# Second expert's weights into the staging tiles, fourth expert's into the tile of the MoE stage freed last, and two small ScalarE stores moved behind a copy

## The chip, the cores and the metric

The kernel runs on one core of a Trainium2 chip, as one launch. The metric is device time in microseconds, the median of the runs shown. Engines are named as in the profile: PE (matmul) with PEld (its weight loads), DVE (VectorE), ACT (ScalarE), POOL (GpSimd) and SP (SyncE, which issues most DMAs). "ACTq", "SPq" and "POOLq" are the queues of these engines where they issue a DMA.

## What is computed

Two layers of a transformer-like trunk on 512 latent and 256 context tokens of width 1024. Each layer has a mixer (projections, a convolution, a state-space scan, an output projection), and then a mixture of experts, which is the part that matters here:

```
t = modulate(rms_norm(h, g_ffn), shift, scale)          # (tokens, 1024)
g_sel = argmax(t @ w_rg + b_rg)                         # one of 4 groups
top_v, top_i = top_k(softmax(expert logits in g_sel), 2)
comb[e, t] = weight of expert e for token t             # two of 16 experts per token
for e in 16 experts:                                    # SwiGLU, hidden width 256
    hid = silu(t @ w_gate[e]) * (t @ w_up[e])
    out += comb[e][:, None] * (hid @ w_down[e])
h = h + gate * out
```

All is float32. Layer 0 routes all 768 tokens, layer 1 (the last) only the 512 latent ones. At the end one RMS norm of the latent tokens is the output.

## The kernel before

**Routing and blocks.** The kernel computes only what the routing chose. Token rows are written to a table in HBM (`h2d`, by `Pair.store`, L1036). From the logits DVE works out which tokens go to which expert; blocks of at most 128 tokens are fetched from `h2d` by an indirect DMA of POOL (`gather`, L1282), turned on PE (`turned`, L1288), copied from PSUM by ACT (first half) and DVE (second half) in `turn` (L1297, the copies are L1301), multiplied by gate and up (`up`, L1315), by silu (`swiglu`, L1309), turned again (`turn_hid`), multiplied by down (`down`, L1343) and added into `acc_d` in HBM by an indirect DMA (`scatter`).

**Experts.** Experts 0, 1 and 2 are "static": their blocks come first, whatever the routing, and they are multiplied in plain float32 straight from the loaded weights. The other 13 come in an order that the routing sets (a register holds the expert's number; `expert`, L1365), and their weights are split into a high and a low part (`split_load`, L1265): ACT casts the loaded piece to the high part (L1275), DVE or POOL subtract for the low part (L1276), and the next expert's piece is loaded in its place. The text calls the fourth expert in order, the first dynamic one, e3, and the next e4.

**Pieces and tiles.** An expert's weights come in six pieces of 512 KB (`load_piece`, L1113): 0 and 1 gate, 2 and 3 up, 4 and 5 down. The tiles are these: `raw0` to `raw5` are the six staging tiles of 4 KB a partition; `HC0`, `HC1` hold expert 0's gate and up; `HL0` and `HL1` are two large tiles (four pieces each) that hold the mixer's activations until the last output projection; `wp` and `wraw` hold down pieces; `C01`, `wraw`, `HL0`, `HL1`, `HC0`, `HC1` later hold high and low parts.

Before, expert 0's gate and up go to HC0 and HC1 and its down to raw4 and raw5; expert 1's gate and up to HL1; expert 2's to HL0; e3's to raw0 to raw3. The large loads after `pr.store` are placed behind the last store by `with behind(pr.stored)` (L1141). e3's pieces are loaded at L1479, once SP has read the number of the expert.

**What sets the order.** The tile framework schedules the program from the source order and its own estimate of time, and each engine then runs its own list strictly in order. Every hardware DMA, from whichever queue, takes the next of eight semaphores in turn; its issue waits until the DMA that had the same semaphore eight places before has landed. So an issue can hold an engine's queue, and everything behind it on that engine, until an unrelated transfer has landed.

**The overflow table.** `loop_rows` (L1457) writes a small table for blocks beyond the planned ones: PE turns it, ACT copies it (L1465), and two stores are issued on ACT's queue, `ovd` (L1468) and `ebd` (L1469). `ebd` needs only `ebi`, which DVE has ready before the first block starts. The loop that reads the table stands at the end of the MoE stage (L1510).

Of the kernel before, what the change touches and what calls it, by code (L numbers as in the profile page):

```python
# [8 lines left out]
F32 = mybir.dt.float32  # L9
# [9 lines left out]
P = 128  # L19
D = 1024  # L20
# [23 lines left out]
def places(caps):  # L44

    static, dyn = caps
    nd = sum(n > P for n in dyn)
    seq, single = [(e, True, n) for e, n in enumerate(static)], list(range(nd, len(dyn)))
    for p in range(nd):
        seq.append((p, False, dyn[p]))  # L50
        k = 0 if p == nd - 2 else -(-len(single) // (nd - p - (p < nd - 2)))
        seq += [(q, False, dyn[q]) for q in single[:k]]
        single = single[k:]
    out, b, row = [], 0, 0
    for p, static, n in seq:
        out.append((p, static, b, row, n))
        b += -(-n // P)
        row += n
    return out
# [3 lines left out]
def hybrid_kernel(ctx: ExitStack, tc: tile.TileContext, x, c, ctxt, c_ctx, w_ada, b_ada, g_mix, g_ffn,  # L63
# [3 lines left out]
    nc = tc.nc  # L67
    V, G, S, T = nc.vector, nc.gpsimd, nc.scalar, nc.tensor

    const = ctx.enter_context(tc.tile_pool(name="const", bufs=1))  # L70
    main = ctx.enter_context(tc.tile_pool(name="main", bufs=1))
# [4 lines left out]
    @contextmanager  # L76
    def behind(*inss):

        with ExitStack() as st:
            for ins in inss:  # L80
                st.enter_context(tc.issue_after(ins.ins))
            yield
# [4 lines left out]
    def tp_tile():  # L87
        return psum.tile([P, 512], F32, name="tp")

    def sm_tile():  # L90
        return psum.tile([P, 512], F32, name="sm")
# [100 lines left out]
    for l in range(2):  # L192
        for p, static, b, row, n in places(CAPS[l]):
            j = p + NE - NS if static else p
# [305 lines left out]
    for l in range(2):  # L500
# [312 lines left out]
        for c in (4, 5, 0, 3, 1, 2):  # L813
            xw = main.tile([P, 2, 512], F32, name="t4", bufs=8)
            G.tensor_mul(v4(xw), hview(xs[:, c, :])[:, None].to_broadcast([P, 2, NH, 64]), both(ex[:, 1], c, 64))
            pt = tp_tile()
# [17 lines left out]
        for i in range(1, 5):  # L834
            for d in range(2):
                c0, c1 = chain[d][i - 1], chain[d][i]
                t = mixp.tile([P, 512], F32, name="Y", bufs=3)
# [231 lines left out]
        def save_x1(i0):  # L1069
            for i in (i0, i0 + 1):  # L1070
                nc.sync.dma_start(out=chunk(acc_d, i + 1), in_=X1[:, :, i, :])
# [21 lines left out]
        items, M_x = places(CAPS[l]), MAXOV[l]  # L1093
# [19 lines left out]
        def load_piece(e, j, t=None):  # L1113

            if t is None:
                t = moep.tile([P, D], F32, name=f"raw{j}")
            w = (w_gate, w_up, w_down)[j // 2]
            src = w[l][e] if isinstance(e, int) else w[l][ds(e, 1)].rearrange("a r f -> (a r) f")
            src = src.rearrange("(p k) f -> p k f", p=P)
            n = src.shape[1] // 2  # L1120
            nc.sync.dma_start(out=t.rearrange("p (k f) -> p k f", k=n), in_=src[:, n * (j % 2):n * (j % 2) + n, :])
            return t


        raw, gu, dn = {}, {}, {}
        t = [main.tile([P, 2048], F32, name=f"HC{q}") for q in range(2)]
        for j in range(4):
            load_piece(0, j, t[j // 2][:, j % 2 * D:j % 2 * D + D])
        gu[0], dn[0] = [t], [[load_piece(0, j) for j in (4, 5)]]
        before = moep.tile([P, 16, 16], F32, name="before")  # L1130
        G.affine_select(out=before, in_=ones[:, 0:1, None].to_broadcast([P, 16, 16]), pattern=[[1, 16], [-1, 16]],
                        compare_op=OP.is_gt, fill=0.0, base=0, channel_multiplier=0)
# [4 lines left out]
        pr.store(nc.sync)  # L1137
        pr.finish()

        t = [main.tile([P, 4, D], F32, name=f"HL{q}") for q in (1, 0)]  # L1140
        with behind(pr.stored):  # L1141
            gu[1] = [[load_piece(1, j, t[0][:, j]) for j in range(4)]]
            dn[1] = [[load_piece(1, j, main.tile([P, D], F32, name="wp", bufs=2)) for j in (4, 5)]]
            if last:
                save_x1(2)
            gu[2] = [[load_piece(2, j, t[1][:, j]) for j in range(4)]]
            t = main.tile([P, 2, D], F32, name="wraw", bufs=3)
            dn[2] = [[load_piece(2, j, t[:, j - 4]) for j in (4, 5)]]


        def rt(name, *shape, dt=F32):
            return moep.tile([P, *shape], dt, name=name)
# [71 lines left out]
        for e in range(NS):  # L1224
# [3 lines left out]
            pt = sm_tile()  # L1228
# [68 lines left out]
        def turn(xg, n, whole):  # L1297
            if whole:
                x = main.tile([P, K8, P], F32, name="t4", bufs=8)[:, :, :n]
                for (ks, pt), copy in zip(turned(xg, n), (S.copy, V.tensor_copy)):  # L1300
                    copy(x[:, ks, :], pt)  # L1301
                return [x]
            xh, xl = [main.tile([P, K8, P], F32R, name="t4", bufs=8)[:, :, :n] for _ in range(2)]
            for ks, pt in turned(xg, n):
                S.copy(xh[:, ks, :], pt)
                V.tensor_sub(xl[:, ks, :], pt, xh[:, ks, :])
            return xh, xl
# [57 lines left out]
        def expert(i):  # L1365
            p, static = items[i][:2]
            return p if static else nc.sync.value_load(eidi[0:1, p:p + 1], min_val=NS, max_val=NE - 1)
# [89 lines left out]
        def loop_rows():  # L1457

            ov = rt("ov", 2, M_x)
            V.tensor_copy(ov[:, 0], idx[:, NB:])  # L1460
            V.tensor_copy(ov[:, 1], cw[:, NB:])
            pt = tp_tile()
            T.transpose(pt[0:2 * M_x, 0:P], ov.rearrange("p q b -> p (q b)"), ident)
            ovT = main.tile([P, P], F32, name="diag", bufs=2)[0:2 * M_x]
            S.copy(ovT, pt[0:2 * M_x, 0:P])  # L1465
            ovd = dram.tile([2 * M_x, P], F32, name=f"ovd{l}")
            ebd = dram.tile([M_x, 1], I32, name=f"ebd{l}")
            nc.scalar.dma_start(out=ovd, in_=ovT)  # L1468
            nc.scalar.dma_start(out=ebd.rearrange("b o -> o b"), in_=ebi[:, :M_x])  # L1469
            return ovd[0:M_x], ovd[M_x:2 * M_x], ebd  # L1470

        blocks = [(i, items[i][2] + j, j == 0) for i in range(NE) for j in range(-(-items[i][4] // P))]
# [3 lines left out]
        whole = lambda w: len(w) == 1  # L1476
        ninc, eidi, bf, rf = slots()
        e3, e4 = expert(3), expert(4)
        raw[3] = [load_piece(e3, j) for j in range(4)]  # L1479
        xT = turn(xgs.pop(0), size[0], whole(gu[0]))  # L1480
        hid, prev_i = None, None
        for i, b, new in blocks:
            if b + 2 == NS:
                idx, cw, ebi = slot_tokens()
# [18 lines left out]
            if new and i == 4:  # L1503
                idxd, cwd, ebd = loop_rows()
# [61 lines left out]
    for i in range(4):  # L1566
        xf = combine(i)
        ss = sml.tile([P, 8], F32, name="ss")
        o = main.tile([P, D], F32, name="t4", bufs=8)
# [36 lines left out]
```

## Time and profile before

| what | value |
|---|---|
| median of 3 runs | 1329.05 us (1326.38 to 1335.55) |
| the profiled execution's own time | 1326.32 us |
| its span, first to last instruction | 1324.6 us |
| PE busy | 1081.6 us (82%) |
| DVE, POOL, ACT busy | 879.0, 611.0, 552.3 us |
| moved by DMA | 259.82 MB, mean 196 GB/s |
| mean granted TensorE clock | 0.912 |

The profile is of one execution. The MoE stage of layer 0 lies from about 473 to 720 us of the span, that of layer 1 from about 1054 to 1300. In each, a routing part (PE nearly idle, DVE at work on small tables, the DMA engines loading weights) is followed by the blocks. A granted clock of 1.00 is 2.4 GHz and 0.50 is 1.2 GHz, its two levels. In a timeline a row gives the start in us, the busy time in us, the engine and line, the operation with its tiles, and in brackets how long the engine sat idle before it and what ended that. A matmul of float32 operands shows as two records, so `x8` of L1320 in the trace is `x4` in the program's order.

### The profile page before, as it was taken

Reading aid. Unit: us, or ns where it says so; the run is one execution under the profiler, and the core shown is the slowest. Engines: PE = TensorE matmul, PEld = TensorE weight load, DVE = VectorE, ACT = ScalarE, POOL = GpSimd, SP = SyncE. Lnnn points to the kernel's source line nnn. Section 1 sums busy time; section 2 is a strip of 40 time slices with the busy share of each in tenths; the row PEclk is TensorE's granted clock in tenths of the full one; section 3 lists DMA queues with packets and bytes.
Section 4 is the critical chain, followed back from the end, with each engine's and each line's share of the span. In section 5 each row is a group of like instructions: output and inputs, shape, how many; then the busy total and the mean of one; then the engine's idle time right before and its main releaser. Section 6 shows DMA issues by size and latency. Waiting matters only on the chain. (4 is left out here: it accounts for less than half of the span.)

```text
span 1324.6 us, 19405 instructions
## 1 busy us (share of the span) xinstructions
PE 1081.6 (82%) x7091; PEld 880.8 (66%) x7091; DVE 879.0 (66%) x1326; ACT 552.3 (42%) x993; POOL 611.0 (46%) x463
## 2 busy tenths in 40 slices
PE   3889697697879958999997498998888948998881
PEld 1567575566769946888885475976667936787750
DVE  3459997668776474477662679975877473476872
ACT  3522243334682322476652422233654212366641
POOL 1427485347683010376763135233865111378761
PEclk9989798897999977999999699889898978999996
DMA  8865433553445175799995746013575275799974
GB/s 265 272 174 182 148 128 91 186 198 95 125 151 139 43 273 199 227 344 333 319 315 112 257 152 217 11 49 121 182 257 204 60 273 202 211 324 315 320 234 138
DMA packets 121360, 259.82 MB, mean 196 GB/s; under 512 B 15968, under 2 KB 61646, under 8 KB 116142
## 3 DMA queue, kind: packets, MB, share of 16 engines
q1 hardware_dynamic: 110852, 227.19, 50.4%
q0 software_dynamic: 8032, 27.14, 8.9%
q10 hardware_dynamic: 2377, 4.22, 0.8%
q8 instruction: 57, 0.93, 0.3%
q14 instruction: 42, 0.34, 0.1%
HBM read 228.05 MB, written 30.47 MB: 195 GB/s over the span
## 5 line engine op out<-in xcount | busy, mean ns | idle before, releaser
L464 POOL TENSOR_TENSOR t<-wp,t 128x1024 fp32r<-128x1024 f32 (+1 forms) x36 | 109.3, 3037 | 149.5 <-ACT t L463 132.9
L723 DVE SCALAR_TENSOR_TENSOR acc<-v,cwcol,acc 128x448 f32<-128x448 f32 (+19 forms) x176 | 131.5, 778 | 0.6
L481 PE MATMUL mm<-HL,t 128*128 128x512 f32 (+1 forms) x272 | 110.6, 409 | 9.3 <-ACT t L463 6.2
L1275 ACT CAST wraw<-raw 128x1024 fp32r<-128x1024 f32 x84 | 87.1, 1049 | 56.7 <-DMA raw<-in_w_gate_dram 21.1
L483 PE MATMUL mm<-HL,t 128*128 128x512 f32 (+1 forms) x272 | 106.6, 392 | 2.2 <-POOL t L464 2.2
L482 PE MATMUL mm<-HL,t 128*128 128x512 f32 (+1 forms) x272 | 107.8, 396 | 0.2 <-DVE HL L376 0.2
L1362 POOL DMA_INDIRECT acc_d<-t,idx x38 | 66.1, 1740 | 84.7 <-issue 22.1
L354 POOL TENSOR_TENSOR rstd<-ms,mhalf 128x1 f32<-128x1 f32 (+3 forms) x29 | 24.5, 846 | 158.8 <-DVE ms L352 134.5
L1284 POOL DMA_INDIRECT t<-h2d,idx x38 | 47.1, 1239 | 95.0 <-PE sm L1320 31.2
L652 DVE SCALAR_TENSOR_TENSOR t<-t,pcol,t 128x772 f32<-128x772 f32 (+1 forms) x64 | 86.9, 1358 | 1.9
L482 PE MATMUL sm<-C,t 128*128 128x256 f32 (+8 forms) x288 | 81.2, 282 | 4.2 <-DVE C L1276 2.5
L481 PE MATMUL mm<-t,HL 128*128 128x256 f32 x256 | 77.0, 301 | 8.6 <-ACT t L644 2.3
L481 PE MATMUL sm<-wraw,t 128*128 128x256 f32 (+8 forms) x288 | 83.6, 290 | 0.0
L1276 POOL TENSOR_TENSOR HL<-raw,HL 128x1024 fp32r<-128x1024 f32 x24 | 64.6, 2725 | 39.1 <-ACT HL L1275 33.7
L483 PE MATMUL sm<-wraw,t 128*128 128x256 f32 (+8 forms) x288 | 80.9, 281 | 0.0
L463 ACT CAST t<-wp 128x1024 fp32r<-128x1024 f32 (+1 forms) x40 | 42.1, 1054 | 90.3 <-DMA wp<-in_w_in_dram 40.0
L483 PE MATMUL mm<-t,HL 128*128 128x256 f32 x256 | 75.3, 295 | 0.1
L482 PE MATMUL mm<-t,HL 128*128 128x256 f32 x256 | 75.2, 294 | 0.0
L1276 POOL TENSOR_TENSOR C<-raw,wraw 128x1024 fp32r<-128x1024 f32 x24 | 62.6, 2620 | 20.6 <-ACT wraw L1275 19.4
L481 PEld LDWEIGHTS mm<-HL,t 128*128 128x128 f32 x272 | 53.5, 198 | 27.0 <-ACT t L463 8.0
L482 PE MATMUL sm<-HL,t 128*128 128x256 f32 (+8 forms) x224 | 63.8, 285 | 4.0 <-DVE HL L1276 3.2
L481 PE MATMUL sm<-HL,t 128*128 128x256 f32 (+8 forms) x224 | 64.2, 287 | 1.3 <-ACT HL L1275 1.3
(468 smaller groups left out, 3383.1 us busy)
## 6 DMA issues: line engine op xcount, KB each, us to landing
wraw<-in_w_ada_dram SPq DMA_DIRECT2D x32, 1024.0 KB
raw<-in_w_down_dram SPq DMA_DIRECT2D x56, 512.0 KB
raw<-in_w_gate_dram SPq DMA_DIRECT2D x52, 512.0 KB
raw<-in_w_up_dram SPq DMA_DIRECT2D x52, 512.0 KB
wp<-in_w_in_dram SPq DMA_DIRECT2D x40, 512.0 KB
wraw<-in_w_ada_dram SPq DMA_DIRECT2D x16, 512.0 KB
wp<-in_w_out_dram SPq DMA_DIRECT2D x16, 512.0 KB
HC<-in_w_ada_dram SPq DMA_DIRECT2D x8, 1024.0 KB
```

Of the source, the lines that this page charges most:

```text
L354: G.tensor_tensor(r[:, :n], ms[:, :n], mhalf[:, :n], op=OP.pow)
L463: S.copy(hi, t)
L464: eng.tensor_sub(lo, t, hi)
L481: T.matmul(dst, lh, rh, start=(k == 0), stop=False)
L482: T.matmul(dst, lh, rl, start=False, stop=False)
L483: T.matmul(dst, ll, rh, start=False, stop=(k == K8 - 1))
L652: V.scalar_tensor_tensor(xa[:, :n], xpt[:, tap:tap + n], col, xa[:, :n], op0=OP.mult, op1=OP.add)
L723: eng.scalar_tensor_tensor(da, sa, tapc(k, ct), da, op0=OP.mult, op1=OP.add)
L1275: highs.append(S.copy(hi, r))
L1276: eng.tensor_sub(lo, r, hi)
L1284: gathered.append(G.indirect_dma_start(out=xg[:n], out_offset=None, in_=h2d, in_offset=bass.IndirectOffsetOnAxis(ap=icol[:n], axis=0)))
L1362: G.indirect_dma_start(out=acc_d, out_offset=bass.IndirectOffsetOnAxis(ap=icol[:n], axis=0), in_=y[:n], in_offset=None, compute_op=OP.add)
```

## The change

Four things are done to both layers' MoE stages:

1. Expert 1's gate and up are loaded to `raw0` to `raw3`, right behind expert 0's down pieces and ahead of the stores of the last `Pair`, instead of to HL1 behind these stores.
2. e3's gate and up are loaded to HL1 instead of raw0 to raw3, still once the expert's number has been read.
3. Expert 2's load keeps HL0.
4. The issues of `ovd` and `ebd` are placed behind the ACT copy that fills `ovd`'s source.

```diff
         gu[0], dn[0] = [t], [[load_piece(0, j) for j in (4, 5)]]
+        gu[1] = [[load_piece(1, j) for j in range(4)]]
...
-        t = [main.tile([P, 4, D], F32, name=f"HL{q}") for q in (1, 0)]
+        room2, room3 = [main.tile([P, 4, D], F32, name=f"HL{q}") for q in range(2)]
         with behind(pr.stored):
-            gu[1] = [[load_piece(1, j, t[0][:, j]) for j in range(4)]]
             dn[1] = [[load_piece(1, j, main.tile([P, D], F32, name="wp", bufs=2)) for j in (4, 5)]]
...
-            gu[2] = [[load_piece(2, j, t[1][:, j]) for j in range(4)]]
+            gu[2] = [[load_piece(2, j, room2[:, j]) for j in range(4)]]
...
-            S.copy(ovT, pt[0:2 * M_x, 0:P])
+            turned = S.copy(ovT, pt[0:2 * M_x, 0:P])
...
-            nc.scalar.dma_start(out=ovd, in_=ovT)
-            nc.scalar.dma_start(out=ebd.rearrange("b o -> o b"), in_=ebi[:, :M_x])
+            with behind(turned):
+                nc.scalar.dma_start(out=ovd, in_=ovT)
+                nc.scalar.dma_start(out=ebd.rearrange("b o -> o b"), in_=ebi[:, :M_x])
...
-        raw[3] = [load_piece(e3, j) for j in range(4)]
+        raw[3] = [load_piece(e3, j, room3[:, j]) for j in range(4)]
```

SP's list in layer 0, from expert 0's down pieces on; before:

```order
L1121 DMA raw4_4012<-in_w_down_dram 128x1024
L1121 DMA raw5_4014<-in_w_down_dram 128x1024
L1041 DMA h2d_209<-wp_3898 128x512 x2
L1041 DMA h2d_209<-wp_3899 128x512 x2
L1121 DMA HL1_4041<-in_w_gate_dram 128x1024 x2
L1121 DMA HL1_4041<-in_w_up_dram 128x1024 x2
L1121 DMA HL0_4042<-in_w_gate_dram 128x1024 x2
L1121 DMA HL0_4042<-in_w_up_dram 128x1024 x2
L1121 DMA wp_4047<-in_w_down_dram 128x1024
L1121 DMA wraw_4055<-in_w_down_dram 128x1024 x2
L1121 DMA wp_4049<-in_w_down_dram 128x1024
```

The same place in the changed kernel (`h2d` are the stores that the first gather waits for):

```order
L1121 DMA raw4_4012<-in_w_down_dram 128x1024
L1121 DMA raw5_4014<-in_w_down_dram 128x1024
L1121 DMA raw0_4016<-in_w_gate_dram 128x1024
L1121 DMA raw1_4018<-in_w_gate_dram 128x1024
L1121 DMA raw2_4020<-in_w_up_dram 128x1024
L1121 DMA raw3_4022<-in_w_up_dram 128x1024
L1041 DMA h2d_209<-wp_3898 128x512 x2
L1041 DMA h2d_209<-wp_3899 128x512 x2
L1121 DMA HL0_4049<-in_w_gate_dram 128x1024 x2
L1121 DMA HL0_4049<-in_w_up_dram 128x1024 x2
L1121 DMA wraw_4059<-in_w_down_dram 128x1024 x2
L1121 DMA wp_4051<-in_w_down_dram 128x1024
```

Four pieces of 512 KB moved from behind the four stores to ahead of them; e3's four loads follow at the end of both lists, behind the same number of bytes. In layer 1 the same move is made.

ACT's list in layer 0, from the routing's last activation to the first silu; before:

```order
L1239 ACTIVATE ev_4190<-v2_4070 128x24
L1469 DMA ebd0_4898<-ebi_4407 1x12
L1301 COPY t4_4325<-tp_4326 128x512
L1275 CAST wraw_4462<-raw0_4317 128x1024
L1275 CAST wraw_4462<-raw1_4319 128x1024
L1275 CAST wraw_4463<-raw2_4321 128x1024
L1301 COPY t4_4349<-tp_4350 128x512
L1275 CAST wraw_4463<-raw3_4323 128x1024
L1311 ACT_TABLE_LOAD
```

The same place in the changed kernel:

```order
L1301 COPY t4_4325<-tp_4326 128x512
L1275 CAST wraw_4462<-HL1_4050 128x1024 x2
L1275 CAST wraw_4463<-HL1_4050 128x1024 x2
L1301 COPY t4_4349<-tp_4350 128x512
L1311 ACT_TABLE_LOAD
L1311 ACTIVATE ad_4370<-sm_4340 128x256
L1336 COPY ad_4423<-sm_4420 128x256
```

The issue of `ebd0` is gone from here, and all four casts of e3 now stand ahead of the copy for the second block (the second L1301). DVE's list changes alike: in layer 0 four subtractions (L1276) and the two L1429 stand ahead of its second L1301, where two subtractions, the two L1429 and one more subtraction stood. In layer 1 the second L1301 of ACT stands behind two casts instead of three:

```order
L1301 COPY t4_9773<-tp_9774 128x4x96
L1275 CAST wraw_9906<-HL1_9533 128x1024 x2
L1301 COPY t4_9797<-tp_9798 128x4x96
L1275 CAST wraw_9907<-HL1_9533 128x1024 x2
L1311 ACT_TABLE_LOAD
```

That is the changed kernel's list; in the one before, `ebd1`'s issue stands ahead of the first L1301 there too. In both layers `ebd` and `ovd` are now issued while the fifth expert's block is under way. Late in layer 1, from the ninth dynamic block on, the order of ACT's casts and token copies (L1305) changes too: for two blocks the token copies move behind the silu of the block before, for two they move ahead of it.

## Rows read from the trace of the kernel before

**Rows 1.** Stretches of 10 and 33 us: busy time by engine, clock, DMA

```profile
core 0: us, PE busy (x) PEld busy (x) DVE busy (x) ACT busy (x) POOL busy (x), PEclk, DMA share, GB/s
500.00:510.00 10.00, 4.74 (x15) 3.51 (x14) 0.69 (x1) 0.79 (x2) 0.00 (x0) 0.50 1.03 412
...
1090.00:1100.00 10.00, 3.65 (x13) 2.65 (x14) 0.56 (x1) 0.48 (x1) 0.00 (x0) 0.50 1.02 356
...
594.00:627.00 33.00, 33.00 (x243) 29.68 (x241) 23.83 (x29) 21.54 (x34) 21.57 (x12) 1.00 1.01 338
...
1188.00:1221.00 33.00, 28.27 (x188) 24.20 (x187) 21.91 (x30) 20.18 (x31) 24.70 (x11) 0.95 1.00 319
```

**Rows 2.** Timeline of ACT, layer 0, first blocks: start, us, operation [idle before]

```profile
504.68 0.53 ACTq L1469 DMA_DIRECT2D ebd<-ebi  x1
505.30 0.58 ACT L1301 COPY t<-tp 128x512 f32<-128x512 f32 x1 [21.88 <-DMA ebd<-ebi]
509.80 1.04 ACT L1275 CAST wraw<-raw 128x1024 fp32r<-128x1024 f32 x1 [3.91 <-DMA raw<-in_w_gate_dram]
...
512.24 1.05 ACT L1275 CAST wraw<-raw 128x1024 fp32r<-128x1024 f32 x1 [0.18 <-DMA raw<-in_w_up_dram]
513.19 0.58 ACT L1301 COPY t<-tp 128x512 f32<-128x512 f32 x1
```

**Rows 3.** Timeline of PE, layer 0: first block turned, experts 0 and 1

```profile
498.71 1.97 PE L1294 MATMUL tp<-ident,t 128*128 128x128 f32 x8 [1.29 <-DMA t<-h2d,idx]
505.94 3.78 PE L1320 MATMUL sm<-HC,t 128*128 128x256 f32 x8 [5.26 <-ACT t L1301]
...
516.52 1.89 PE L1320 MATMUL sm<-HL,t 128*128 128x256 f32 x8
...
518.68 1.89 PE L1320 MATMUL sm<-HL,t 128*128 128x256 f32 x8
```

**Rows 4.** DMA rate from 470 to 560 us, 40 slices of 2.25 us

```profile
GB/s 39 7 246 373 366 271 400 411 419 419 415 410 408 411 406 411 421 406 109 2 0 0 0 0 0 75 377 286 310 320 271 359 20 0 144 89 117 262 293 344
```

**Rows 5.** Timelines of SP and POOL, layer 0: stores, next loads, first gather

```profile
478.76 2.31 SPq L1041 DMA_DIRECT2D h2d<-wp  x4
481.12 2.21 SPq L1121 DMA_DIRECT2D HL<-in_w_gate_dram  x2
...
490.83 1.24 POOL L1284 DMA_INDIRECT t<-h2d,idx  x1 [12.89 <-DMA HL<-in_w_up_dram]
```

**Rows 6.** Timeline of DVE, layer 0, between the first two blocks

```profile
513.23 1.82 DVE L1429 TENSOR_TENSOR t<-iota,rf 128x768 bf16<-128x768 f32 x2
...
516.10 0.68 DVE L1301 COPY t<-tp 128x512 f32<-128x512 f32 x1
516.70 1.21 DVE L1276 TENSOR_TENSOR C<-raw,wraw 128x1024 fp32r<-128x1024 f32 x1
```

**Rows 7.** Two stretches of 1 us after PE stopped (columns as in rows 1)

```profile
480.00:481.00 1.00, 0.01 (x1) 0.00 (x0) 1.00 (x4) 0.00 (x0) 0.00 (x0) 0.85 1.11 414
...
1074.00:1075.00 1.00, 0.00 (x0) 0.00 (x0) 0.93 (x7) 0.12 (x1) 0.00 (x0) 0.81 1.07 285
```

**Rows 8.** Timeline of ACT, layer 1, first block

```profile
1097.23 0.48 ACT L1301 COPY t<-tp 128x384 f32<-128x384 f32 x1 [22.14 <-DMA ebd<-ebi]
1101.79 1.04 ACT L1275 CAST wraw<-raw 128x1024 fp32r<-128x1024 f32 x1 [4.08 <-DMA raw<-in_w_gate_dram]
```

**Rows 9.** Timeline of PE, layer 1: first block turned, experts 0 and 1

```profile
1089.87 1.54 PE L1294 MATMUL tp<-ident,t 96*128 96x96 f32 x8 [2.71 <-DMA t<-h2d,idx]
1097.76 3.73 PE L1320 MATMUL sm<-HC,t 128*96 128x256 f32 x8 [6.35 <-ACT t L1301]
...
1107.53 1.89 PE L1320 MATMUL sm<-HL,t 128*96 128x256 f32 x8
...
1109.67 1.89 PE L1320 MATMUL sm<-HL,t 128*96 128x256 f32 x8
```

**Rows 10.** DMA rate from 1050 to 1140 us, 40 slices of 2.25 us

```profile
GB/s 7 23 380 195 273 403 128 0 11 164 355 171 395 419 392 413 354 262 299 308 410 410 411 404 22 11 0 0 0 35 260 269 253 269 308 315 162 0 42 191
```

## Prediction

> **What bounds the kernel now.** I read the timelines of PE and ACT at the head of each layer's blocks first, since the change touches what ACT does there. In layer 0 PE turns the first block at 498.71 and then sits idle 5.26 us, until 505.94, for ACT's copy of that block [rows 3]. The copy (0.58 us) is itself late only because ACT sat 21.88 us behind the issue of `ebd`, at 504.68, a store that nobody needs yet [rows 2]. Layer 1 repeats it: turned at 1089.87, copy at 1097.23 after 22.14 us behind `ebd`, matmuls at 1097.76 after 6.35 us of waiting [rows 8, 9]. The issue of `ebd` waits for an old load that had the same semaphore, so it moves with the weight stream, and the matmuls with it.
>
> The stretch table comes next, since time won there must survive to the end. From 594 to 627 PE is busy 33.00 of 33 us: layer 0's blocks are bound by PE, and an earlier start passes through. From 1188 to 1221 PE has 28.27 of 33 us while the DMA share is 1.00: late layer 1 waits for weights [rows 1]. These loads are issued in order as tiles come free, so they start earlier if the first blocks end earlier; I count layer 1's gain in full too.
>
> Last come the rates of the DMA engines. In layer 0 they run at 400 to 420 GB/s from about 481 to 511, without a hole. In layer 1 there is a hole: 128, 0 and 11 GB/s from 1063.5 to 1070.25, between expert 0's weights and the last stores [rows 4, 10].
>
> **The change, layer 0.** *The stores.* They were issued from 478.76, with HL1's pieces from 481.12 behind them [rows 5]. Now four pieces, 2.1 MB, lie ahead of them. Expert 0's six pieces (3.15 MB), the four new ones and the four stores (1.05 MB) are 6.29 MB. Summed from 474.5 on, the rates give 5.6 MB by 490.25 and 6.5 MB by 492.5 [rows 4]; so the stores have moved at about 491.9, and I allow 1.1 us (an estimate) until they are seen: 493. The first gather went out at 490.83 [rows 5], its list just ready, so it slips to about 493.3, by 2.5 us, and the turning from 498.71 to 501.2.
>
> *The copy.* With `ebd` gone ACT copies as soon as the first half is turned, about 1 us later: 502.2 to 502.8 (0.58 us). PE starts expert 0 at 502.85, 3.1 us ahead of 505.94 [rows 2, 3].
>
> *What is late next.* Expert 0 takes 516.52 − 505.94 = 10.6 us [rows 3], partly at the low clock, so it ends at 513.4. The second block needs ACT's second copy, which stood behind three casts of e3 and now stands behind four. The casts run as the pieces land: 509.80 and 512.24 are the first and third [rows 2], so 1.22 us apart, the fourth at about 513.46. The same bytes lie ahead of these pieces as before and the stream has no hole to fill [rows 4], so these times stay. Fourth cast 513.46 to 514.5 (1.05 us), second copy to 515.0 (0.58). PE starts expert 1 at 515.0, not 516.52, after about 1.6 us of waiting.
>
> Its second group also needs DVE's copy, now behind the fourth subtraction (1.21 us) and the two L1429 (1.82): 514.5 + 1.21 + 1.82 + 0.68 = 518.2 [rows 6]. Before, the second group started at 518.68 [rows 3]. **Layer 0 gains 0.5 us**, not 3.1: 1.6 of it goes to the wait for the fourth cast, the rest to DVE. Bounds: 3.1 if the second copies were not held, −1.4 if the stop in front of expert 1 costs PE its clock (second rival).
>
> **The change, layer 1.** The stores depend on DVE's work and stay at about 1070.5, where the rate rises again [rows 10]. The tiles raw0 to raw3 are long free and the semaphores of their loads belong to small stores ahead, so the four loads go out right behind expert 0's and take 2.1 MB / 410 GB/s = 5.1 us of the hole, to about 1069.6. The stores and the gather don't move, the turning stays at 1089.87, and ACT's copy can run at about 1090.7. PE starts at 1091.3 instead of 1097.76: 6.5 us earlier [rows 9].
>
> Here the second copies do not hold it. From 1070.25 to 1104 the stream moved 11.6 MB (the rates summed); now 2.1 MB of them are already there, so e3's pieces land 5.1 us earlier: the first at 1101.79 − 5.1 = 1096.7, then 1.22 us apart to 1100.4 [rows 8, 10]. ACT's second copy stands behind two casts: 1097.9 + 1.05 + 0.48 = 1099.4. PE needs it at 1091.3 + (1107.53 − 1097.76) = 1101.1 [rows 9]. DVE's copy stands behind three subtractions and the two L1429; the third cast runs behind ACT's copy, 1099.4 to 1100.45, the subtraction takes 1.21 us more and the copy at most 0.68: 1102.4. The second group wants it at 1109.67 − 6.47 = 1103.2. **Layer 1 gains 6.4 us**, bounds 4.0 (the copy on DVE 1.2 us late, and the clock rising as much later) and 7.5 (rising earlier).
>
> **The clock in between.** Both first groups of expert 0 run at the low level: 3.78 and 3.73 us, against 1.89 for the same eight matmuls at the high one [rows 3, 9]. Starting earlier doesn't change that, since PE idled ahead of it in either case.
>
> **Edits at nothing.** `ovd` and `ebd` now issue in the fifth expert's block, 0.53 us on ACT each [rows 2]. ACT is busy 21.54 of 33 us in such a stretch [rows 1], so they hide; without that cover they cost 0.53 us a layer each. Behind `ebd` on ACT would stand that block's copies, if it had to wait for a semaphore; loads of eight places before are landed by then. The load of e4 into raw0 to raw3 must now wait for expert 1's matmuls, but stands on SP behind the loads into raw4 and raw5, which wait longer. The new order of ACT late in layer 1 moves two blocks' copies behind a silu and two ahead: I take zero. Its bound is a cast pair, 2 x 1.05 us, for two blocks: 4.2 us lost.
>
> **The sum.** 0.5 + 6.4 = 6.9 us, against the profiled execution's 1326.32 (its span is 1324.6, the rest lies around it): 1319.4. The median of the runs, 1329.05, is 2.7 us above the profiled one; on that basis 1322.1, rounded to 1322.
>
> **The rivals.**
> *1. Layer 0 gains fully.* The early stream of layer 0 shows 246, 373, 366 and 271 GB/s [rows 4]: with four more loads queued these slices could reach 410: (4 x 410 − 1256) x 2.25 us = 0.86 MB, or 2.1 us of stream. Stores, gather and e3 would all come 2.1 us earlier, and layer 0 would gain 2.6, with the copies out of the way 5.2. Total up to 11.6: 1317.5. For: more transfers in flight. Against: the slow slices belong to expert 0's pieces, which were queued as fast as SP could.
>
> *2. The clock falls in layer 0's new stop.* PE stops at about 513.4 with the clock high, and starts again at 515.0. If expert 1's first group then runs as expert 0's did, 3.78 instead of 1.89 us, layer 0 loses 1.4 instead of gaining 0.5: total 5.0, 1324. The trace has the clock down soon after two stops: 0.85 in the mean from 480 to 481, and 0.81 from 1074 to 1075 [rows 7]. But PE had worked little just ahead of these; at 513 it has worked for over 10 us.
> The Trainium skill, "TensorE: Matmul & The Clock Gate", section "HAM oscillation — how this bites in real kernels", speaks for this rival: it says that a wait for DMA between groups of matmuls can make each next group start at the low clock. By it the total would be 5.0; rows 7 agree that stops lower the clock, and no row shows a stop of this length behind a full stretch.
>
> *3. Late layer 1 gives it back.* That stretch is at DMA share 1.00 [rows 1]; if the earlier start doesn't reach the loads, or the new order of ACT costs its 4.2 us, 2.7 us or less remain: 1326.4.
>
> *4. Slower: the stores of layer 0 land only with the end of the stream.* If the 16 DMA engines share their time among all queued transfers instead of taking the stores in order, the stores end when the stream does, at about 511 [rows 4], the gather follows at 512, the matmuls of expert 0 at 521.8: 15.9 us late. With layer 1's 6.4 that is 9.5 lost: 1338.6. It decides from a gather that is some 12 us late on; layer 0 alone breaks even when expert 0 starts at about 505.4. Against: before, the stores lay behind expert 0's 3.15 MB and ahead of HL1's, and the gather went out by 490.83, with 20 us of stream still to come [rows 4, 5]: they land in order.
>
> That the change does nothing is no case of its own: `ebd` is no longer ahead of the copy in either list.
>
> **How the numbers follow.** The forecast has 0.55, rival 1 0.13, rival 2 0.15, rival 3 0.12, rival 4 0.05. The bounds of the two layers (−1.4 to 3.1 and 4.0 to 7.5) give gains of 2.6 to 10.6 us, 1318.5 to 1326.5; rival 1 extends that to 1317.5, rival 3 stays inside. The runs of before spread from 1326.38 to 1335.55, so the median itself may lie some 4 us to either side of this basis: 1314 to 1331. About 1% (13.3 us) is what a measurement of this kernel can tell from no change, so the forecast counts as the same: faster needs rival 1 with a low median or a later gain I don't see (0.08), slower needs rival 4 with more added (0.04), same 0.88.
>
> **What would show it.** In ACT's timeline the first L1301 should be ended by PE or the gather, not by `ebd`, and `ebd` should stand in the fifth expert's block, 0.5 us long. Layer 0: gather at about 493.3, expert 0 from 502.9, casts from HL1 from 509.8 on, ACT's second copy at 514.4, PE idle from 513.4 to 515.0, expert 1's second group at 518.2. Layer 1: the rate between 1063.5 and 1070.25 near 400, gather unmoved, expert 0 at 1091.3, e3's first cast at about 1096.7, expert 1's second group at 1103.2. I am wrong if the gather of layer 0 comes after 500, if e3's pieces come later than 513.5 there, or if layer 1's late loads do not start some 6 us earlier than before.

## The result, and the profile after

The changed kernel takes 1317.97 us (median of 9 runs, 1313.44 to 1323.85) against 1331.03 us (9 runs, 1325.99 to 1335.55): a ratio of 0.9907, 95% interval 0.988 to 0.9934. That is 12 us, 9 to 16 by the interval (the two medians are 13.1 us apart), where 6.9 were forecast. The time lies in the forecast range; the sum lies below the interval. The profiled execution took 1321.23 us (span 1319.5), one of the slower ones. In it the routing of layer 0 comes 0.90 us later than in the profile before and that of layer 1 4.77 us later (the same matmuls of the routing, L1202 and L1064, compared); times below that are compared with before have this taken off.

The timeline of ACT after, in layer 0: start, us, operation [idle before].

```profile
504.33 0.59 ACT L1301 COPY t<-tp 128x512 f32<-128x512 f32 x1 [19.99 <-PE tp L1294]
509.39 1.04 ACT L1275 CAST wraw<-HL 128x1024 fp32r<-128x1024 f32 x1 [4.48 <-DMA HL<-in_w_gate_dram]
...
513.77 1.04 ACT L1275 CAST wraw<-HL 128x1024 fp32r<-128x1024 f32 x1 [0.19 <-DMA HL<-in_w_up_dram]
514.72 0.58 ACT L1301 COPY t<-tp 128x512 f32<-128x512 f32 x1
...
571.81 0.53 ACTq L1470 DMA_DIRECT2D ebd<-ebi  x1
```

The copy now follows PE, not `ebd`, which is issued in 0.53 us in the fifth expert's block. PE and POOL in the same place:

```profile
503.12 1.97 PE L1294 MATMUL tp<-ident,t 128*128 128x128 f32 x8 [4.80 <-DMA t<-h2d,idx]
504.96 7.01 PE L1320 MATMUL sm<-HC,t 128*128 128x256 f32 x22
...
515.36 1.99 PE L1320 MATMUL sm<-raw,t 128*128 128x256 f32 x8 [0.34 <-ACT t L1301]
...
518.47 2.00 PE L1320 MATMUL sm<-raw,t 128*128 128x256 f32 x8 [0.68 <-DVE t L1301]
```

```profile
495.21 1.24 POOL L1284 DMA_INDIRECT t<-h2d,idx  x1 [16.36 <-DMA HL<-in_w_gate_dram]
```

Against [rows 3, 5], and with 0.90 off: the gather at 494.3 instead of 490.8, expert 0 at 504.1 instead of 505.9, expert 1's second group at 517.6 instead of 518.7. PE waits 0.34 and 0.68 us there for the second copies. The DMA rates from 470.9 to 560.9 us, so that the slices are those of [rows 4]:

```profile
GB/s 40 13 244 390 408 382 417 362 398 419 416 419 411 410 410 413 410 348 42 0 0 0 0 0 0 167 355 255 335 295 295 311 4 0 228 35 138 271 319 353
```

With four more loads queued, the slices that had 373, 366 and 271 GB/s have 390, 408 and 382. Layer 1, PE and then ACT:

```profile
1094.22 1.54 PE L1294 MATMUL tp<-ident,t 96*128 96x96 f32 x8 [2.29 <-DMA t<-h2d,idx]
1095.75 3.73 PE L1320 MATMUL sm<-HC,t 128*96 128x256 f32 x8
...
1105.37 1.89 PE L1320 MATMUL sm<-raw,t 128*96 128x256 f32 x8
...
1108.42 1.97 PE L1320 MATMUL sm<-raw,t 128*96 128x256 f32 x8 [0.75 <-DVE t L1301]
```

```profile
1095.22 0.48 ACT L1301 COPY t<-tp 128x384 f32<-128x384 f32 x1 [15.36 <-PE tp L1294]
1102.05 1.04 ACT L1275 CAST wraw<-HL 128x1024 fp32r<-128x1024 f32 x1 [6.35 <-DMA HL<-in_w_gate_dram]
...
1104.21 0.47 ACT L1301 COPY t<-tp 128x384 f32<-128x384 f32 x1
```

With 4.77 off, against [rows 8, 9]: the turning at 1089.45 (1089.87), expert 0 at 1090.98 (1097.76), e3's first cast at 1097.3 (1101.8), expert 1's second group at 1103.65 (1109.67). The hole of [rows 10] is full: the DMA rates of the same 90 us, in slices of 2.25 us, are now

```profile
GB/s 0 0 7 4 352 219 254 416 417 412 270 117 381 379 212 315 415 417 280 280 282 306 413 388 78 4 0 0 0 177 249 239 273 315 277 322 20 0 180 53
```

417, 412 and 270 GB/s from 1068 to 1074.75, where on before's clock 128, 0 and 11 stood. So far this is the forecast. Two things in the trace are not. First, layer 0 loses 6 us near 661 of before's clock, where PE waits 3.60 us for a gather and goes on at the low clock:

```profile
666.05 1.05 PE L1294 MATMUL tp<-ident,t 32*128 32x32 f32 x8 [3.60 <-DMA t<-h2d,idx]
```

```profile
667.00:668.00 1.00, 1.00 (x5) 0.97 (x5) 0.53 (x2) 0.86 (x2) 0.00 (x0) 0.50 1.02 401
```

Second, layer 1 gains once more late in its blocks. From the matmul at 1188.1 in the profile before to the one at 1289.3 (some 580 PE operations) it takes 101.20 us before and 95.70 after. The table of stretches, before and then after (columns as in rows 1: PE, PEld, DVE, ACT, POOL busy, clock, DMA share, GB/s):

```profile
1188.10:1289.30 101.20, 86.75 (x579) 70.22 (x579) 72.93 (x83) 59.88 (x83) 75.69 (x32) 0.98 0.93 295
```

```profile
1187.70:1283.40 95.70, 87.08 (x581) 70.05 (x580) 68.51 (x84) 58.83 (x81) 69.50 (x32) 0.98 0.95 308
```

The operations are the same. PE sits idle 8.6 us instead of 14.5, and the DMA engines move 308 instead of 295 GB/s. I call this the late stretch below. Layer 0's own late stretch, 594 to 627, is as in [rows 1]: PE 32.89 of 33 us.

### The profile page after: what moved, and what is told of

Read it like the earlier page. It is cut to its first block, busy times and chain, and to the rows that moved or that the text cites. A ratio compares the mean times of both kernels' runs of the same rounds, so it can differ in the third digit from the quotient of the medians.

```text
span 1319.5 us, 19390 instructions
## 1 busy us (share of the span) xinstructions
PE 1083.4 (82%) x7091; PEld 881.7 (67%) x7091; DVE 878.5 (67%) x1326; ACT 552.7 (42%) x993; POOL 606.7 (46%) x463
## 5 line engine op out<-in xcount | busy, mean ns | idle before, releaser
L481 PE MATMUL mm<-HL,t 128*128 128x512 f32 (+1 forms) x272 | 109.3, 404 | 10.0 <-ACT t L463 6.0
L483 PE MATMUL mm<-HL,t 128*128 128x512 f32 (+1 forms) x272 | 105.7, 389 | 1.2 <-POOL t L464 1.2
L482 PE MATMUL mm<-HL,t 128*128 128x512 f32 (+1 forms) x272 | 106.6, 392 | 0.0
L1275 ACT CAST wraw<-raw 128x1024 fp32r<-128x1024 f32 x76 | 78.4, 1048 | 41.4 <-DMA raw<-in_w_down_dram 12.9
L483 PE MATMUL sm<-wraw,t 128*128 128x256 f32 (+8 forms) x288 | 81.1, 282 | 0.0
L1276 POOL TENSOR_TENSOR HL<-raw,HL 128x1024 fp32r<-128x1024 f32 x24 | 59.5, 2518 | 43.3 <-ACT HL L1275 36.8
L1276 POOL TENSOR_TENSOR C<-raw,wraw 128x1024 fp32r<-128x1024 f32 x24 | 60.8, 2544 | 29.5 <-ACT wraw L1275 27.3
```

The costliest lines, as they stand in the source:

```text
L481: T.matmul(dst, lh, rh, start=(k == 0), stop=False)
L482: T.matmul(dst, lh, rl, start=False, stop=False)
L483: T.matmul(dst, ll, rh, start=False, stop=(k == K8 - 1))
L1275: highs.append(S.copy(hi, r))
L1276: eng.tensor_sub(lo, r, hi)
```

## The experiments

Three theories for the gain. **Theory 1**: the sum of the prediction, a head start at each layer's first blocks, limited by the second copies. **Theory 2**: the wait for `ebd` was the whole cause. **Theory 3, later theory O**: part of the gain is the new order of PE, DVE and ACT late in layer 1, which the scheduler chose anew when the loads moved. Against O stands **H**: the late stretch is shorter because the weights got a head start. **Theory 4** is on the loss near 661: an accident of one execution. Runs are named by e1 to e11; e3 and e4 alone are experts, as before, and the runs with these numbers have their full names.

### One part of the change alone

`e1_stores_only` keeps all tiles:

```diff
-            S.copy(ovT, pt[0:2 * M_x, 0:P])
+            turned = S.copy(ovT, pt[0:2 * M_x, 0:P])
-            nc.scalar.dma_start(out=ovd, in_=ovT)
-            nc.scalar.dma_start(out=ebd.rearrange("b o -> o b"), in_=ebi[:, :M_x])
+            with behind(turned):
+                nc.scalar.dma_start(out=ovd, in_=ovT)
+                nc.scalar.dma_start(out=ebd.rearrange("b o -> o b"), in_=ebi[:, :M_x])
```

> Only the issues of ovd and ebd are moved behind the ACT copy; all weights go to the tiles they had before. Theory 1 (the sum of the prediction: the gain stands at the head of the blocks and is limited by the second block's copies): expert 0 starts 5.2 us earlier in layer 0 (500.7) and 6.4 earlier in layer 1 (1091.4), but the second copies stay behind the casts of e3, which land as before. ACT's second copy lets expert 1 start at 513.8 and 1105.7, DVE's second copy lets its second group start at 516.8 (518.68 before) and 1109.25 (1109.67 before): gains of 1.9 and 0.4 us, together 2.3 us, a ratio of 0.998. Theory 2 (the wait for ebd is the whole cause, and the second copies don't hold it): 5.2 + 6.4 = 11.6 us, 0.991. Theory 3 (what was gained beyond the sum, some 5 us, came late in layer 1 with the new order of ACT there): as theory 1, 0.998, since this kernel keeps the old order late in layer 1.

Measured: 1.0017 (0.9997 to 1.0038), nothing gained. Removing 22 us of idle time on ACT in each layer bought nothing, and PE's timeline in layer 1 shows why; ACT's rows, from the same profile, stand below it (its routing is 3.04 us later than in the profile before):

```profile
1094.33 3.73 PE L1320 MATMUL sm<-HC,t 128*96 128x256 f32 x8
...
1108.59 3.59 PE L1320 MATMUL sm<-HL,t 128*96 128x256 f32 x8 [4.43 <-ACT t L1301]
...
1112.43 1.89 PE L1320 MATMUL sm<-HL,t 128*96 128x256 f32 x8
```

```profile
1104.63 1.04 ACT L1275 CAST wraw<-raw 128x1024 fp32r<-128x1024 f32 x1 [10.35 <-DMA raw<-in_w_gate_dram]
...
1107.12 1.04 ACT L1275 CAST wraw<-raw 128x1024 fp32r<-128x1024 f32 x1 [0.24 <-DMA raw<-in_w_up_dram]
1108.07 0.47 ACT L1301 COPY t<-tp 128x384 f32<-128x384 f32 x1
```

Expert 0 starts 6.5 us earlier (1094.33 − 3.04 = 1091.3), then PE stops 4.43 us for the second copy, which stands behind three casts of e3 that land when they always did. The stop costs the clock as well: the group behind it takes 3.59 us, the next one 1.89. At expert 1's second group 0.3 us are left of 6.5. Theory 2 falls. Theory 1 had 0.4 us for this place. In layer 0 it had 1.9 us. There PE stops 3.40 us for the second copy, and expert 1's second group comes 1.0 us earlier than in the first profile of before, but 0.5 to 1.0 us later than in six other profiles whose layer 0 is unchanged (`e4_before_again`, e5, e6, e9, e10 and e11 below). Theory 1's whole, 0.998, lies just below the interval, so its 2.3 us did not come either.

`e2_tiles_only` is the other half: the change without `with behind(turned)`.

```diff
-            with behind(turned):
-                nc.scalar.dma_start(out=ovd, in_=ovT)
-                nc.scalar.dma_start(out=ebd.rearrange("b o -> o b"), in_=ebi[:, :M_x])
+            nc.scalar.dma_start(out=ovd, in_=ovT)
+            nc.scalar.dma_start(out=ebd.rearrange("b o -> o b"), in_=ebi[:, :M_x])
```

> Only the tiles and the place of expert 1's load are changed; ovd and ebd are issued where they were before. ebd still holds ACT's first copy. Theory 1: layer 0 as before (the stream ends when it did, the copy comes at about 505.3): 0 us; in layer 1 the load whose semaphore ebd waits for lands 5.1 us earlier, so copy and expert 0 come about 5 us earlier (1092.6 counted on the before's clock), and the second copies follow: 5 us, ratio 0.996. Theory 2 (the wait for ebd is the whole cause and stays): 0 to 1 us, 0.999 to 1.000. Theory 3 (the new order of ACT late in layer 1, which this kernel has, brings some 5 us): 5 + 5 = 10 us, 0.9925.

Measured: 0.9915 (0.9884 to 0.9946): all of the gain, as theory 3 had it. The head of layer 1 gains 6.2 us, not 5. I had expected `ebd` to hold the first copy still; it doesn't:

```profile
1092.07 0.49 ACTq L1469 DMA_DIRECT2D ebd<-ebi  x1
1095.34 0.48 ACT L1301 COPY t<-tp 128x384 f32<-128x384 f32 x1 [15.78 <-PE tp L1294]
```

The routing is 4.47 us later in this profile, so `ebd` goes out at 1087.6 on before's clock instead of 1096.64, ahead of the turning. In layer 0 of the same profile it goes out at 499.91, ahead of the turning at 501.99. Once the loads lie earlier, the semaphore it waits for is free in time. The fourth item of the change had nothing left to do in either layer.

`e6_l1_both` makes the whole change in layer 1 alone (first diff), `e7_l0_both` in layer 0 alone (with `not last`), and in both the stores of `ovd` and `ebd` move only there. `e8_tiles_behind` exchanges the tiles in both layers but leaves expert 1's loads behind the stores, and `ovd` and `ebd` where they were (second diff):

```diff
+        early = last
+        if early:
+            gu[1] = [[load_piece(1, j) for j in range(4)]]
...
-        raw[3] = [load_piece(e3, j) for j in range(4)]
+        raw[3] = [load_piece(e3, j, room3[:, j]) if early else load_piece(e3, j) for j in range(4)]
```

```diff
         with behind(pr.stored):
-            gu[1] = [[load_piece(1, j, t[0][:, j]) for j in range(4)]]
+            gu[1] = [[load_piece(1, j) for j in range(4)]]
...
-        raw[3] = [load_piece(e3, j) for j in range(4)]
+        raw[3] = [load_piece(e3, j, room3[:, j]) for j in range(4)]
```

> The whole change, in layer 0 alone; layer 1 as before, with ebd ahead of its copy and the old order late. The prediction's step: 0.5 us gained, ratio 0.9996, expert 0 some 2 to 3 us earlier against the routing, expert 1's second group 0.5 to 1 us earlier, late stretch of layer 1 107 us. Rival for layer 0 (the change loses some 3 us between 523 and 720): ratio 1.002. If the whole gain came from layer 0's part in some way: 0.991.

> The whole change, in layer 1 alone; layer 0 as before. Theories O and H: the head of layer 1 gains 6 to 6.6 us as in the changed kernel, the late stretch takes 100 to 102 us: 12 us in all, ratio 0.991. If the prediction's step for layer 0 holds (0.5 us gained there), this kernel is 0.5 us slower than the changed one; rival for layer 0 (the change loses some 3 us there: from 523 to 720 the kernels with the change lost 4.0 to 7.0 us against the first profile of before, those without it 2.4 and 3.5): it is 2 to 3 us faster than the changed kernel, 0.989.

> The tiles are exchanged as in the change, in both layers, but expert 1's loads stay behind the stores, and ovd and ebd stay where they were. The order late in layer 1 is the old one, and the hole in the stream of layer 1 stays. If the place of the loads ahead of the stores (head start in layer 1) and the new late order carry the gain: ratio 1.000 within 0.2%, ebd holding the first copy as before, late stretch 107 us. If the exchange of the tiles itself carries it (e3's loads no longer waiting for a staging tile): 0.991 to 0.995.

Measured: layer 0 alone 0.999 (0.9968 to 1.0012), layer 1 alone 0.9916 (0.9884 to 0.9947), tiles exchanged behind the stores 0.9983 (0.9964 to 1.0002). The gain is layer 1's, and it needs the loads ahead of the stores. Layer 0 gives nothing that can be measured: the 0.5 us of theory 1 cannot be told from nothing, while a loss of 3 us (ratio 1.002) lies outside the interval.

### The spread between executions

`e3_after_again` and `e4_before_again` are the two kernels once more, unedited.

> The changed kernel once more, for a second profiled execution. Theory 1 and theory 3: the same ratio as measured, 0.988 to 0.993, and the head of the blocks in each layer as in the first profile: expert 0 1.9 us earlier in layer 0 and 6.8 in layer 1 against the routing before it. Theory 4: the 6 us that the first profile lost near 661 of layer 0 (PE waited 3.6 us for a gather and went on at the low clock) is an accident of that execution, and is absent here; if it belongs to the change, it stands here too, at the same block.

> The kernel before once more, for a second profiled execution and as a measure of the spread. Ratio 1.000 within 0.3% either way. Theory 4 (executions differ by accidents of a few us where PE loses its clock behind a late gather or load): the second profile differs from the first by such a place in the blocks or in the mixer, while expert 0 waits for ebd in both, 5.3 and 6.4 us.

Measured: 0.9934 (0.9911 to 0.9957) and 1.0007 (0.9984 to 1.0029). The loss near 661 is absent from the second profile of the changed kernel, so it is no part of the change. In the first, POOL's issue of a gather had taken 5.76 us:

```profile
650.15 5.76 POOL L1284 DMA_INDIRECT t<-h2d,idx  x1 [0.16 <-issue]
```

Its rows landed 15.8 us after the issue began, and PE's matmul at 666.05 had to wait for them; in the first profile of before the same gather took 0.89 us and landed after 5.4. In the second profile of the changed kernel it took 0.89:

```profile
653.62 0.89 POOL L1284 DMA_INDIRECT t<-h2d,idx  x1 [0.15 <-issue]
```

The spread is not small: the second profile of before took 1337.80 us, the first 1326.32. Both have the same wait ahead of expert 0 in layer 1, 6.35 and 6.33 us. Of the 11.5 us between them 5.4 arise between expert 1's second group in layer 0 and the routing of layer 1, and 5.2 behind the late stretch. Between 523 and 719 the first profile of before, the one that the prediction was read from, was the quickest of all thirteen: the others took 2.0 to 7.0 us longer there, whether changed in layer 0 or not.

### Order or head start

Late in layer 1 these kernels have one of two orders. It is the new one as soon as one piece of 512 KB lies ahead of the stores, and the old one again if a needless load of 512 KB is put in behind them. That allows both crossings. `e5_l1_early1` (and `e10_early1_again`, the same kernel) has the new order with a quarter of the head start (first diff, against e6); `e9_l1_dum1` (and `e11_dum1_again`) has the old order with three quarters of it (second diff, against e6):

```diff
-            gu[1] = [[load_piece(1, j) for j in range(4)]]
+            gu[1] = [[load_piece(1, j) for j in range(1)]]
...
         with behind(pr.stored):
+                gu[1][0] += [load_piece(1, j) for j in range(1, 4)]
```

```diff
         with behind(pr.stored):
+            if early:
+                for j in range(1):
+                    load_piece(1, j, room3[:, j])
```

> Layer 1 alone is changed, and only one of expert 1's four pieces is loaded ahead of the stores (0.5 MB into the hole of the stream instead of 2.1 MB); the other three go to their staging tiles behind the stores. Every engine but SP has the very order of e6, late in layer 1 too. Theory O (the order of PE, ACT and DVE late in layer 1 is worth some 6 us of its own: the same 602 PE operations from 1188 to 1295 took 106.7 to 107.4 us in three profiles with the old order and 99.7 to 102.1 in three with the new): the head gains less, since e3 lands only 1.3 us earlier (0.52 MB at 410 GB/s), DVE's second copy comes at about 1106 and expert 1's second group 3.6 us earlier than before; the late stretch still takes 100 to 102 us; total 9 to 10 us, ratio 0.993. Theory H (the late stretch is shorter because weights have a head start there): the stretch takes 105 to 107 us, total 3.6 + 1.5 = 5 us, ratio 0.996.

> e5 once more (one piece of four in the hole, the new late order), since its first profile was of one of its slowest executions: there the head gained 2.6 us and the stretch from 1188 to 1289 (before's clock) was 2.5 us shorter than before, against 4.4 to 7.1 with all four pieces. Theory O: 4 to 7 us shorter here, ratio 0.993 again. Theory H: 0 to 1.5 us shorter, ratio 0.996. Both together, half each: 2 to 3.5 us shorter, ratio 0.995.

> As e6 (the whole change in layer 1 alone, all four pieces of expert 1 in the hole of the stream), with one piece of 512 KB more: it is loaded twice, once uselessly to HL1 behind the stores, before e3 overwrites it. e3 so lands 1.6 MB / 410 GB/s = 3.8 us earlier than before instead of 5.1. With this load the scheduler gives back the old order of PE, ACT and DVE late in layer 1. Head: ACT's second copy behind three casts at 1102, DVE's behind four subtractions at 1104.9, on before's clock: 4.8 us gained at expert 1's second group. Theory O (the order late in layer 1 is worth some 5 us of its own): the 602 PE operations from 1188 to the last down (106.7 to 107.4 us with the old order, 99.7 to 102.1 with the new) take 106 to 107.5; total 5 us, ratio 0.996. Theory H (a head start of the weights alone shortens that stretch): 102 to 103 us; total 9 us, ratio 0.993.

> e9 once more, for a second profile of the old late order with most of the head start. Theory O: the stretch from 1188 takes 106 to 107.5 us. Theory H: 102 to 103 us. The ratio as in e9.

In the traces, from 1188 of before's clock to the end of the late stretch, e9 and e11 run the lists of before on every engine, e5 and e10 those of the change; the lists of POOL and SP are the same there in all thirteen profiles.

Measured, with all kernels that have either order. "Head" is what expert 1's second group in layer 1 gains against the routing ahead of it, compared with the first profile of before; the late stretch is between the same two matmuls in all.

| kernel | moved ahead | order late in layer 1 | head, us | late stretch, us | ratio |
|---|---|---|---|---|---|
| before | none | old | 0 | 101.2 | 1 |
| `e4_before_again` | none | old | 0.0 | 101.4 | 1.0007 |
| e1, stores only | none | old | 0.3 | 101.9 | 1.0017 |
| e7, layer 0 alone | none in layer 1 | old | 0.3 | 100.5 | 0.999 |
| e8, tiles behind | none | old | −0.1 | 100.3 | 0.9983 |
| e9 | 4 pieces, less 1 | old | 4.5 | 101.7 | 0.9953 |
| e11, as e9 | 4 pieces, less 1 | old | 3.5 | 101.8 | 0.9979 |
| e5 | 1 piece | new | 2.6 | 98.7 | 0.993 |
| e10, as e5 | 1 piece | new | 2.7 | 95.4 | 0.9934 |
| the change | 4 pieces | new | 6.0 | 95.7 | 0.9907 |
| `e3_after_again`, as the change | 4 pieces | new | 6.6 | 94.1 | 0.9934 |
| e2, tiles only | 4 pieces | new | 6.2 | 96.6 | 0.9915 |
| e6, layer 1 alone | 4 pieces | new | 6.6 | 96.9 | 0.9916 |

The seven profiles with the old order take 100.3 to 101.9 us, the two with a large head start among them; the six with the new order take 94.1 to 98.7, the two with a small head start among them. H falls and O holds: the order is worth 5.4 us in the mean of the four profiles with all four pieces (101.2 less 95.8). The clock is not the reason: before, e8 and e9 have 0.98 in this stretch and take 100.3 to 101.7 us, and e10, the change and e6 have 0.98 and take 95.4 to 96.9. The stretch of e11, then of e10:

```profile
1188.70:1290.50 101.80, 89.84 (x580) 72.83 (x580) 71.17 (x83) 58.70 (x81) 77.48 (x32) 0.95 0.92 292
```

```profile
1190.20:1285.60 95.40, 86.93 (x581) 70.24 (x580) 69.76 (x84) 58.31 (x81) 70.53 (x32) 0.98 0.97 311
```

The head follows the pieces, and less than in step. By theory 1 e5 should gain 3.6 and did 2.6 us; e9 should gain 4.8 and did 4.5 and 3.5. The ratios of e9 and e11 are 6.2 and 2.8 us of 1329.7, about the head alone (intervals 0.9935 to 0.9972 and 0.9953 to 1.0005). In their two profiles, though, only 1.5 and 0.8 us of the head are left where the late stretch begins: from expert 1's second group to there they take 81.3 and 81.1 us, against 78.2 to 80.3 in the five profiles with no piece moved ahead. Why stays open. Those of e5 and e10 are 9 us (0.9904 to 0.9957 and 0.9911 to 0.9958), of which 2.6 of head and 2.5 and 5.8 of late stretch are found in the profiles; e5's profile is of its slowest execution, 1332.21 us.

Why the new order is faster can be shown only in part. SP's waits in the late stretch of before and of the changed kernel (what its issues waited for: us in all, times, longest):

```profile
SPq L1121 <- POOL C L1276: 16.5, 7, 3.0
SPq L1121 <- POOL HL L1276: 15.9, 8, 2.8
...
SPq L1121 <- DVE t L1306: 6.3, 2, 3.2
```

```profile
SPq L1121 <- POOL HL L1276: 14.3, 8, 2.0
SPq L1121 <- POOL C L1276: 13.4, 7, 2.9
...
SPq L1121 <- DVE t L1306: 3.8, 3, 2.1
```

In all seven profiles with the old order the loads wait 6.3 to 10.1 us at the token subtractions of DVE (L1306), in the six with the new one 3.8 to 4.9, and the DMA share is 0.91 to 0.93 against 0.93 to 0.97. The subtractions that the loads wait for (L1276) are shorter too. They alone, in the late stretch before and then after (DVE and POOL busy, clock, DMA share, GB/s):

```profile
1188.10:1289.30 101.20, 53.57 (x34) 46.71 (x17) 0.98 0.93 295
```

```profile
1187.70:1283.40 95.70, 47.86 (x33) 41.69 (x17) 0.98 0.95 308
```

The 16 that start on POOL in the stretch take 43.5 to 45.9 us in the profiles with the old order and 40.5 to 42.7 in those with the new. I read this as staging tiles that come free with shorter gaps when the turning of the later tokens stands differently between casts and subtractions; that reading is argued and not shown. Which of the moved instructions does it was not tried and stays open.

## Why the prediction was right, and where its sum was not

**The head of layer 1, right.** 6.4 us were forecast, with the gather unmoved, the hole filled, e3's first cast 5.1 us earlier and expert 1's second group at 1103.2. Measured: 6.0 to 6.6 in four profiles, the cast 4.5 us earlier, the group at 1103.65. Two misses of the sum partly cancel in this: expert 1's first group came at 1100.6 (1101.1 forecast), and DVE's copy, which the sum had ready by 1102.4 with 0.8 us to spare, ended at 1103.6, so that PE waited 0.75 us for it. PE begins the late stretch 4.8 to 6.7 us earlier against the routing in these four, where some 6 us were forecast for the late loads.

**The head of layer 0, a term within the noise.** The stores had landed at 493.2, as the sum had it (493, with 1.1 us that were worked out from no row), but the gather slipped to 494.3 (493.3 forecast). Expert 0 came 1.2 us later than forecast and the second group 0.6 earlier. Against the profile it was read from the term looks under-sized (1.1 us, 0.5 forecast). But the six other profiles with an unchanged layer 0 were 1.5 to 2.0 us quicker up to that group than the one the sum was read from, and the four with the loads moved there (the change in both its profiles, e2 and e7) 0.5 to 2.1; so against those the change gains nothing, and the ratio of layer 0 alone agrees. One execution was taken for the kernel.

**"I take zero" for the new order late in layer 1: this step failed.** It was looked at on ACT alone, as four moved token copies, with a bound of 4.2 us on the side of a loss and none on the side of a gain. PE's and DVE's lists had changed there too, and the stretch was known to have DMA share 1.00 and PE at 28.27 of 33 us [rows 1]: a place where a shift in when staging tiles come free can move the end. The mis-sized term is 0 for a measured 5.4 us. With 6.4 and about 0 for layer 0 it makes 11.8, inside the interval of the result. The profiles show somewhat less: from the routing of layer 1 to the end of the span the four with all four pieces take 235.8 to 240.0 us, the first of before 248.2. How much of the head alone reaches the end is open: e9 and e11, which have it without the new order, take 246.9 and 248.4 us.

**The range held by its allowance.** The bounds of the two layers gave at most 10.6 us, or 1318.5, and 11.6 us, or 1317.5, with rival 1, whose gain did not come. The measured 1317.97 lies between these, and the medians are 13.1 us apart. So the time lies safely in the range only by the 4 us or so that were added for the spread of the median, and not because a term allowed for the gain that came. That part is luck.

**The rivals.** Rival 1's condition came in part: in the four slow slices of layer 0's early stream (the last, 481.25 to 483.5, was also read into the 400 to 420 GB/s) 0.38 MB more were moved, not 0.86, and e3's first cast came 1.3 us earlier than in the first profile of before, 0.4 earlier than in its second, not 2.1; but the gather was later, and nothing was gained.

Rival 2 did not come in either profile of the changed kernel. Its stop in layer 0 was 0.34 us in the first and 1.59 in the second, where the sum had 1.6, and the group behind it took 1.99 us in both. But its mechanism exists at about this length: in e2 a stop of 1.94 us in the same place is followed by a group of 2.85. The second profile of the change, then e2:

```profile
517.00 1.99 PE L1320 MATMUL sm<-raw,t 128*128 128x256 f32 x8 [1.59 <-ACT t L1301]
```

```profile
514.54 2.85 PE L1320 MATMUL sm<-raw,t 128*128 128x256 f32 x8 [1.94 <-ACT t L1301]
```

e1 shows it where the stop is longer: 4.43 us, then 3.59 us for a group of 1.89. What the prediction held against this rival was misread: ahead of the stops of [rows 7] PE had not worked little, but 4.41 of 5 us from 475 to 480 and 4.69 of 5 from 1065 to 1070. The Trainium skill, "TensorE: Matmul & The Clock Gate", section "HAM oscillation — how this bites in real kernels", says that a wait for DMA between groups of matmuls can start the next at the low clock; the trace agrees for the stops of 1.94 us in e2 and of 3.40 and 4.43 us in e1 (waits for ACT's copy here), and not for the other stops ahead of expert 1's first two groups, the longest of them 2.05 us in e5.

Rival 3 named the right place with the wrong sign. Rival 4 falls: the stores landed in order, and the gather slipped 3.5 us.

**`ebd`.** The prediction began from the 22 us that ACT stood behind it. That wait was real, but the next one on that path took back all but 0.3 us (e1), and the loads alone removed it (e2). What carried the head was the earlier landing of e3's pieces, with the copies behind them.

## What to carry to other kernels

A wait that is removed is worth what the next one on the same path leaves: 6.5 us at expert 0 became 0.3 at expert 1, since casts stood ahead of the next copy on the same in-order engine. Where a scheduler rewrites the order of a stage that is bound by transfers, that order is a term of its own, on every engine and in either sign; here it was nearly half of the gain, and two kernels that cross it with the intended effect, each profiled twice, were enough to tell the two apart. Read a term of 1 us from several executions, not from one.

## What the runs showed of the hardware that was not expected

- The issue of one gather on POOL took 5.76 us in one execution and 0.89 in another of the same kernel, and its rows landed 15.8 us after the issue began; by PE's wait of 3.60 us and its low clock behind it this cost 6 us.
- Executions of one kernel differ by up to 11.5 us in their profiles (1326.32 and 1337.80 for before). Only 2.4 us of this lie between 523 and 719 us of layer 0.
- Ahead of expert 1's first two groups of eight matmuls, stops of PE of up to 2.05 us left the group at 1.97 to 2.00 us (1.89 without a stop), but one of 1.94 us in e2 made it 2.85; stops of 3.40 and 4.43 us in e1 made it 3.11 and 3.59 us. So the length of a stop alone does not tell whether the clock falls.
- With the list of PE, ACT and DVE in another order, the subtractions of the late stretch took 53.57 us on DVE and 46.71 on POOL, or 47.86 (one fewer) and 41.69.
